# The RWKV stage's projections as three fp32r products, with both parts kept in DRAM

## The chip, the cores and the metric

One core of a Trainium2 chip. The time is device microseconds of one execution of the whole program, the median of three runs: 3976.36 us (3972.51 to 3979.13). Engines: TensorE (PE, its weight loads PEld), VectorE (DVE), ScalarE (ACT), GpSimd (POOL) and SyncE (SP), which issues all DMAs from one queue, in order.

## The reference, cut to what matters

One step of a bidirectional hybrid trunk of two layers, on 128 context tokens and 1024 latent tokens (T = 1152 columns in all), in float32, with D = 1024:

```
def trunk_layer(x, mod, p, states, rows, rope):
    h = rmsnorm(x, norm_g) * (1 + scale) + shift            # adaLN
    u = h @ w_in                                            # 1024 -> P_IN, split into four groups
    y_a = mlstm_branch(u_a)       # 4 pairs of heads each
    y_b = rglru_branch(u_b)       # LRU
    y_c = retention_branch(u_c)
    y_d = rwkv_branch(u_d)        # r, k, v, g, and a low-rank part
    x = x + gate * (concat(y_a, y_b, y_c, y_d) @ w_out)     # 4 x 512 -> 1024
```

Each branch runs a recurrence in both directions over the tokens. The result is the last `x` after a final norm, and the context's states.

## The kernel before, in words

Activations lie as [128 features, T tokens]. The token axis is cut into three chunks of `CH3` = 384 columns. A layer has three parts.

*Input projection and three mixers.* `in_proj` makes every column tile of `u` that the first three mixers need, and those of RWKV's pair 0, in the order of the table `JOBS`. The norm leaves `h` in SBUF as two fp32r parts, `hh` and `hl`; a weight tile is loaded and split into `wring_h` and `wring_l`; each product is three fp32r matmuls (hi·hi, hi·lo, lo·hi), accumulated in PSUM: 4032 of them a layer. The tiles of `u` go to DRAM. `ml_pair`, `lr_pair` and `rt_pair` (mLSTM, LRU, retention; pairs 0 to 3 each, written in this order) read them there as they come, at a higher priority than `in_proj`. Each ends with one [128, T] tile of its result, which is stored to DRAM at `yc(m, p)`. Most of a mixer's tiles have one buffer, so its pairs follow each other; retention's pools open where the LRU's close.

*RWKV stage.* `rw_all` goes through nine units (two halves of four pairs, and one for the context). Its chain of steps on TensorE and VectorE has a fixed order on TensorE (`strict`, `chain`), and between the steps `pull` takes "fills" from the generator `work`: one `fill` is one fp32 matmul of 384 columns for one k. Fills make RWKV's own projections for pairs 1 to 3 (`late_proj`, k = 8) and the output projection (`out_proj`, first for the three mixers' 12 k tiles, then for RWKV's pairs 0 to 2), in layer 0 also the remaining modulation rows (`wmod`). Each fill's activations (`y_tile`) and weights (`w_tile`) come from DRAM, through rings of `YOB` and `OWB` buffers. 648 fills a layer, modulation aside.

*Tail.* RWKV's pair 3 is projected with the split done in place (`tail`), then the norm of the next layer or the final one.

Where instructions have no fixed order, the scheduler orders each engine's queue once, when the program is built, by priority, by its estimate of when operands are ready and by when a tile's buffer is free. A pool's buffers are handed out in the order in which the code asks for them. On the chip every queue runs in that order.

Of the kernel before, what the change touches and what calls it, by code (L numbers as in the profile page):

```python
# [19 lines left out]
KT = 8  # L20
# [10 lines left out]
class B:  # L31
# [326 lines left out]
    def rw_final(self, l, X):  # L358

        c, y, W = self.c, X["y"], X["W"]  # L360
        H = [slice(o, o + 512) for o in range(0, W, 512)]
        z = self.rf.tile([128, NST], F32, tag="yq", name="yq")[:, :W]
        for h in H:
            self.act(z[:, h], y[:, h], ACT.Square)
        self.headsum(lambda ps, h: self.act(z[:, h], ps, ACT.Ln, scale=1.0 / 64, bias=c["eps"]), z, W)
        self.act(z, z, ACT.Exp, scale=-0.5)
        for h in H:
            self.tt(self.v if X["p"] == 3 else self.g, z[:, h], z[:, h], X["A"][:, h], MUL)
            self.stt(self.v, z[:, h], z[:, h], 0.5, y[:, h], MUL, MUL)
            self.tt(self.v, y[:, h], z[:, h], X["B"][:, h], ADD)  # L370
            for p, s in X["segs"]:
                a, b = max(s.start, h.start), min(s.stop, h.stop)
                if a < b:
                    o = X["src"].start - s.start
                    self.dma(self.Y[l, 3, p][:, a + o:b + o], y[:, a:b])

    def silu2(self, t, g, out=None):

# [292 lines left out]
    def tok_norm_gate(self, pool, ps, y, p, m, gname, k2, tags, pt_tag):  # L671

        c = self.c
        sq = pool.tile([128, 18, 64], F32, tag=tags[0], name="nsq")
        yv = y.rearrange("p i (h d) -> p (i h) d", d=64)
        self.act(sq, yv, ACT.Square)
        ss = pool.tile([128, 18], F32, tag="nss", name="nss")
        self.v.tensor_reduce(out=ss, in_=sq, op=ADD, axis=AXX)
        self.act(ss, ss, ACT.Ln, scale=1.0 / (64 * k2 * k2), bias=c["eps"])
        self.act(ss, ss, ACT.Exp, scale=-0.5)  # L680
        self.tt(self.g, yv, yv, ss[:, :, None].broadcast_to([128, 18, 64]), MUL)
        g = pool.tile([128, T], F32, tag=tags[1], name="ng")
        self.dma(g, self.uc(gname, p))
        sg = sq.rearrange("p a d -> p (a d)")
        self.silu2(sg, g)
        for i0, n in ((0, 4), (4, 4), (8, 1)):
            pt = ps.tile([128, 512], F32, tag=pt_tag, name="ntr")
            for i in range(n):
                self.t.transpose(pt[:, 128 * i:128 * i + 128], y[:, i0 + i], c["ident"])
            s = slice(128 * i0, 128 * (i0 + n))  # L690
            self.stt(self.v, g[:, s], pt[:, :128 * n], 0.5 / k2, sg[:, s], MUL, MUL)
        self.dma(self.yc(m, p), g)


    def load_consts(self, pool, names):
# [314 lines left out]
    def lr_pair(self, l, p):  # L1010
# [46 lines left out]
        sg = tl("tr")  # L1057
        self.silu2(sg, g)
        self.stt(self.v, hd[0], hd[0], 0.5, sg, MUL, MUL)
        self.dma(self.yc(1, p), hd[0])  # L1060


    def open_main(self):
# [24 lines left out]
            self.par[n] = t  # L1088
        self.mod = [p.tile([128, 24, 2], F32, name="mod%d" % l) for l in range(2)]

    def mod_rows(self, l, j, pool, w, n, pr, pc, mm, between=lambda k: None):


        row_ps = pr()
        for k in range(0, 8, n):
            wt = w()
            self.dma(wt, self.i["w_mod"][l, j][:, k:k + n])
            between(k // n)
            for z in range(n):
                mm(row_ps[0:2], self.sc[:, k + z], wt[:, z], start=(k + z == 0), stop=(k + z == 7))  # L1100
                if k + z < 7:
                    yield
        row = pool.tile([2, 512], F32, tag="mrow", name="mrow", bufs=1)
        self.a.copy(row, row_ps[0:2])
        col_ps = pc()[:, 0:8].rearrange("p (i c) -> p i c", c=2)
        for i in range(4):
            self.tr(col_ps[:, i], row[:, 128 * i:128 * i + 128])
        self.tt(self.v, self.mod[l][:, 4 * j:4 * j + 4], col_ps,
                self.par["bmod"][:, 24 * l + 4 * j:24 * l + 4 * j + 4, None].broadcast_to([128, 4, 2]), ADD)
        yield  # L1110

    def modulation(self, l, j, pool):

        w = lambda: pool.tile([128, 1, 512], F32, tag="ow", name="wmod")
        yield from self.mod_rows(l, j, pool, w, 1, self.pmain, self.pmain, self.fill)

    def modulation0(self, pool, ps, between):

# [13 lines left out]
    def norm_h(self, l, xs, sg, r, hh, hl, o):  # L1132
# [10 lines left out]
                self.tt(e, hl[:, m, s], x, hh[:, m, s].bitcast(F32), SUB)  # L1143
        s = slice(o, o + CH3)
        if o == 0:
            self.H[l] = self.dr0.tile([128, KT, T], F32, name="h_%d" % l)
        self.dma(self.H[l][:, :, s], xs)

    def first_norm(self, hh, hl):
        with ExitStack() as st:  # L1150
# [27 lines left out]
    def tail(self, l, ks, open_h):  # L1178
# [3 lines left out]
        with ExitStack() as st:  # L1182
# [10 lines left out]
            yr = [tp.tile([128, CH3], F32, name="t_yr%d" % j) for j in range(3)]  # L1193
# [9 lines left out]
            for o in range(0, T, CH3):  # L1203
                c = slice(o, o + CH3)
                yh, yl = yt[o // CH3 % 2]
                for j, k in enumerate(ks):
                    raw = yr[(o // CH3 * nk + j) % 3]
                    self.dma(raw, self.Y[l, 3, k][:, c])
                    self.a.copy(yh[:, j], raw)
                    self.tt(self.v, yl[:, j], raw, yh[:, j].bitcast(F32), SUB)  # L1210
# [36 lines left out]
        self.a.copy(hi, raw)  # L1247
        self.tt(self.g, lo, raw, hi.bitcast(F32), SUB)

    def in_proj(self, l, wp, sp, hh, hl):  # L1250
        n = 0
        rh = wp.tile([128, 3, KT, 128], F32R, name="wring_h")
        rl = wp.tile([128, 3, KT, 128], F32R, name="wring_l")
        pos = 0
        for t_, (kind, name, p, tiles) in enumerate(JOBS):
            if name[:3] == "rw_" and p in LATE:
                continue
            nt = len(tiles)
            if pos + nt > 3:
                pos = 0  # L1260
# [35 lines left out]
        return self.pe(self.t.matmul(*a, **k))  # L1296

    def y_tile(self, yp, src):
        t = yp.tile([128, CH3], F32, tag="y", name="yt")
        self.dma(t, src)  # L1300
        return t

    def w_tile(self, wp, src, n=4):
        t = wp.tile([128, 4, 128], F32, tag="ow", name="ow")
        self.dma(t[:, :n], src)
        return [t[:, k] for k in range(n)]

    def proj(self, ws, ys):

        ps = self.pmain()  # L1310
        for k, (w, y) in enumerate(zip(ws, ys, strict=True)):
            self.fill(ps[:, :CH3], w, y, start=(k == 0), stop=(k == len(ws) - 1))
            if k < len(ws) - 1:
                yield
        return ps[:, :CH3]

    def late_proj(self, l, pair, wp, yp, sp):

        js = [(name, tiles[0]) for kind, name, p, tiles in JOBS if name[:3] == "rw_" and p == pair]
        for name, t in js:  # L1320
            self.U[l, name, pair] = self.dr0.tile([128, T], F32, name="u_%s_%d_%d" % (name, pair, l))
        for o in range(0, T, CH3):
            c = slice(o, o + CH3)
            ys = [self.y_tile(yp, self.H[l][:, k, c]) for k in range(KT)]
            for name, t in js:
                ws = sum((self.w_tile(wp, self.i["w_in"][l, t][:, z:z + 4]) for z in (0, 4)), [])
                xi = sp.tile([128, CH3], F32, tag="x", name="xi")
                ps = yield from self.proj(ws, ys)
                self.a.copy(xi, ps)
                self.dma(self.U[l, name, pair][:, c], xi)  # L1330
                yield
        self.done.add(pair)

    def out_proj(self, l, gs, wp, yp, sp):

        X = [self.dr0.tile([128, T], F32, name="x_%d_%d_%d" % (l, gs[0][0], m)) for m in range(8)]
        for o in range(0, T, CH3):
            c = slice(o, o + CH3)
            ys = [self.y_tile(yp, self.Y[l, g, k][:, c]) for g, n in gs for k in range(n)]
            for m in range(8):  # L1340
                ws = sum((self.w_tile(wp, self.i["w_out"][l, g, m][:, 0:n], n) for g, n in gs), [])
# [17 lines left out]
    def build(self):  # L1359
# [10 lines left out]
        for l in range(2):  # L1370
            self.uc = lambda n, p: self.U[l, n, p]
            self.ut = self.uc
            def yc(m, p):
                self.Y[l, m, p] = self.dr0.tile([128, T], F32, name="y_%d_%d_%d" % (m, p, l))
                return self.Y[l, m, p]
            self.yc = yc
            with self.ph as ph:
                P = lambda n, b=1, **kw: ph.enter_context(tc.tile_pool(name=n + "_%d" % l, bufs=b, **kw, **tw))
                wp, sp = P("w"), P("st")
                self.in_proj(l, wp, sp, *self.h)  # L1380
                with tc.high_priority(offset=HP1), ExitStack() as st:
                    Q = lambda n, b=1, **kw: st.enter_context(tc.tile_pool(name=n + "_%d" % l, bufs=b, **kw, **tw))
                    self.mlrow = self.dr.tile([2, 40, T], F32, tag="mlrow", name="mlrow")
# [23 lines left out]
            with ExitStack() as ph:  # L1407
# [9 lines left out]
                def work():  # L1417
                    for p in LATE:
                        for z, j in MODS[p] if l == 0 else ():
                            yield from self.modulation(z, j, wp)  # L1420
                        yield from self.late_proj(l, p, wp, yp, sp)
                    yield from self.out_proj(l, ((0, 4), (1, 4), (2, 4)), wp, yp, sp)
                    while self.finished < 4:
                        yield
                    yield from self.out_proj(l, ((3, 3),), wp, yp, sp)
                    self.done.add("all")

                self.fills, self.done, self.credit, self.pulled, self.finished = work(), set(), 0.0, 0, 0
# [13 lines left out]


LATE, PROMPTS = (1, 2, 3), 6
OWB, SO = 6, 3
MODS = {1: ((0, 4), (0, 5)), 2: ((1, 0), (1, 1), (1, 2)), 3: ((1, 3), (1, 4), (1, 5))}
T12 = 2
LDB = dict(ld=2, ld2=2, y=1)
HP1 = 1000000
HP2 = 2000000  # L1450
RIGHT = "right"
MLB = 1
YOB = 16
RESERVE = 44
HV = (slice(0, 64), slice(64, 128))

# [154 lines left out]
```

## Time and profile before

| | us |
|---|---|
| median of three runs | 3976.36 |
| the profiled execution | 3979.25 |
| its span, first to last instruction | 3977.5 |
| TensorE busy | 3648.6 (92%) |
| VectorE busy | 2033.8 (51%) |
| ScalarE busy | 1291.7 (32%) |
| GpSimd busy | 1110.7 (28%) |
| mean DMA rate | 135 GB/s |

A busy share is a mean over stretches with different limits; matmuls are pipelined and their ends are modelled, so the time from one start to the next is a matmul's cost where they follow each other. In the list of groups one fp32 fill counts as two instructions.

### The profile page before, as it was taken

The page shows a single profiled execution, that of the slowest core. Times are in us where ns is not written, and L with a number is a line of the kernel's source. Part 1 is how long each engine was busy: PE and PEld are TensorE (multiplying, and loading weights), DVE is VectorE, ACT ScalarE, POOL GpSimd, SP SyncE. Part 2 cuts the span into 40 slices and gives each one's busy share as a digit, 9 for nine tenths or more (in the row PEclk, how much of TensorE's full clock was granted, in tenths as well). Part 3 has the DMA queues.
Part 4 walks back from the last instruction along what each step waited for, and adds up shares of the span by engine and source line. Part 5 has one row for each costly group of instructions (what it writes and reads, how often), then busy time and mean ns, then how long its engine had stood idle before and what let it go on. Part 6 is the DMA issues. An engine that isn't in the chain of part 4 may idle for free. (4 is left out here: it accounts for less than half of the span.)

```text
span 3977.5 us, 69524 instructions
## 1 busy us (share of the span) xinstructions
PE 3648.6 (92%) x28050; PEld 2831.0 (71%) x28050; DVE 2033.8 (51%) x3953; ACT 1291.7 (32%) x2102; POOL 1110.7 (28%) x1016
## 2 busy tenths in 40 slices
PE   6899999999899999998888999999997899989997
PEld 2899889999654555555468888999996555655554
DVE  4445544332364566675364545443423566766644
ACT  3234432212223334332142434422121334343313
POOL 4233234424331222212032232344243312122200
PEclk7999899989799999999989998999897999999998
DMA  5434343433356544344653443435333444434446
GB/s 214 122 106 137 121 132 120 141 111 120 127 156 187 146 141 134 109 124 123 198 189 118 104 120 124 129 121 146 106 122 119 133 151 133 141 101 126 129 128 201
DMA packets 413550, 538.02 MB, mean 135 GB/s; under 512 B 141708, under 2 KB 322700, under 8 KB 413228
## 3 DMA queue, kind: packets, MB, share of 16 engines
q1 hardware_dynamic: 413228, 533.57, 44.5%
q8 instruction: 221, 3.62, 0.4%
q14 instruction: 101, 0.83, 0.1%
HBM read 387.17 MB, written 146.25 MB: 134 GB/s over the span
## 5 line engine op out<-in xcount | busy, mean ns | idle before, releaser
L1296 PE MATMUL main<-yt,ow 128*128 128x384 f32 x2592 | 989.0, 520 | 25.1 <-DVE xi L48 17.5
L1296 PEld LDWEIGHTS main<-yt,ow 128*128 128x128 f32 x2592 | 478.0, 197 | 328.0 <-issue 49.1
L59 PE MATMUL main<-hh,wring_h 128*128 128x384 f32 x1824 | 648.1, 356 | 25.6 <-DVE st L1290 11.5
L59 PE MATMUL main<-hl,wring_h 128*128 128x384 f32 x1824 | 647.8, 355 | 21.7 <-DVE hl L44 19.6
L59 PE MATMUL main<-hh,wring_l 128*128 128x384 f32 x1824 | 644.1, 353 | 0.0
L44 POOL TENSOR_TENSOR wring_l<-raw,wring_h 128x1024 fp32r<-128x1024 f32 x100 | 246.8, 2472 | 605.1 <-ACT wring_h L1247 457.7
L59 PEld LDWEIGHTS main<-hh,wring_h 128*128 128x128 f32 x1824 | 360.8, 198 | 39.0 <-DVE st L1290 10.1
L59 PEld LDWEIGHTS main<-hl,wring_h 128*128 128x128 f32 x1824 | 361.1, 198 | 33.8 <-DVE hl L44 22.4
L59 PEld LDWEIGHTS main<-hh,wring_l 128*128 128x128 f32 x1824 | 360.7, 198 | 8.7 <-issue 2.7
L59 PE MATMUL main<-wring_h,hh 128*128 128x256 f32 x864 | 265.0, 307 | 17.7 <-DVE st L1290 17.1
L59 PE MATMUL main<-wring_h,hl 128*128 128x256 f32 x864 | 261.2, 302 | 0.0
L59 PE MATMUL main<-wring_l,hh 128*128 128x256 f32 x864 | 260.4, 301 | 0.0
L44 POOL TENSOR_TENSOR t<-s_k,bb 128x512 f32<-128x512 f32 x36 | 62.4, 1734 | 570.4 <-ACT bb L56 570.4
L1290 DVE COPY st<-main 128x384 f32<-128x384 f32 (+1 forms) x168 | 86.0, 512 | 261.8 <-PE main L59 222.5
L44 DVE TENSOR_TENSOR tm<-iU,iN 64x31 f32<-64x31 f32 (+15 forms) x558 | 202.2, 362 | 15.9
L44 DVE TENSOR_TENSOR iN<-iN,tm 64x31 f32<-64x31 f32 (+15 forms) x558 | 193.8, 347 | 15.8
L59 PEld LDWEIGHTS main<-wring_h,hh 128*128 128x128 f32 x864 | 178.0, 206 | 22.9 <-DVE st L1290 18.5
L59 PEld LDWEIGHTS main<-wring_h,hl 128*128 128x128 f32 x864 | 178.5, 207 | 4.5 <-issue 1.1
L59 PEld LDWEIGHTS main<-wring_l,hh 128*128 128x128 f32 x864 | 178.2, 206 | 2.7
L1247 ACT CAST wring_h<-raw 128x1024 fp32r<-128x1024 f32 x100 | 103.5, 1047 | 221.0 <-PE main L59 178.5
L1288 ACT COPY st<-main 128x384 f32<-128x384 f32 (+1 forms) x168 | 73.4, 437 | 270.2 <-PE main L59 264.3
L56 ACT ACT_TABLE_LOAD x123 | 157.8, 1283 | 2.9 <-PEq L1603 0.7
(332 smaller groups left out, 6040.2 us busy)
## 6 DMA issues: line engine op xcount, KB each, us to landing
raw<-in_w_in SPq DMA_DIRECT2D x100, 512.0 KB
ow<-in_w_in SPq DMA_DIRECT2D x144, 256.0 KB
ow<-in_w_out SPq DMA_DIRECT2D x144, 256.0 KB
yt<-h SPq DMA_DIRECT2D x144, 192.0 KB
mrb<-mlrow SPq DMA_DIRECT2D x48, 384.0 KB
x<-xi SPq DMA_DIRECT2D x96, 192.0 KB
yt<-y SPq DMA_DIRECT2D x90, 192.0 KB
wmod<-in_w_mod SPq DMA_DIRECT2D x64, 256.0 KB
```

The lines of the kernel that those rows point to most:

```text
L44: return e.tensor_tensor(out=out, in0=a, in1=b, op=op)
L56: return self.a.activation(out=out, in_=a, func=f, scale=scale, bias=bias)
L59: return self.t.matmul(out, l, r, start=start, stop=stop)
L1247: self.a.copy(hi, raw)
L1288: self.a.copy(q[:, :w], ps[:, :w])
L1290: self.v.tensor_copy(q[:, :w], ps[:, :w])
L1296: return self.pe(self.t.matmul(*a, **k))
```

## The change

The fp32 fill becomes three fp32r matmuls, whose parts are made once and kept in DRAM.

- `norm_h` stores `hh` and `hl` in place of `h`; the DRAM tile has a part axis.
- The three mixers store through the new `put_y`: a cast to fp32r in a tile of the new pool `yh` (one buffer), a subtraction in place, two stores. `rw_final` does the same by halves.
- `split_work` splits the 56 weight pieces a layer that the fills use; `in_proj` takes two a job.
- `y_tile` and `w_tile` load both parts; the rings become 10 and 4 buffers of twice the size.
- The output projection's groups are 8 and 7 k tiles (mLSTM and LRU, then retention and RWKV's pairs 0 to 2) in place of 12 and 3.
- `t12` and the RWKV loads `ld` go from two buffers to one; the modulation row uses a buffer of the weight ring; the tail loads the two parts.

```diff
@@ rw_final
+            hi, lo = z[:, h].bitcast(F32R), y[:, h].bitcast(F32R)
+            self.a.copy(hi, y[:, h])
+            self.tt(self.v, lo, y[:, h], z[:, h], SUB)
...
@@ tok_norm_gate, and the same in lr_pair with self.put_y(1, p, hd[0])
-        self.dma(self.yc(m, p), g)
+        self.put_y(m, p, g)
@@ norm_h
-            self.H[l] = self.dr0.tile([128, KT, T], F32, name="h_%d" % l)
-        self.dma(self.H[l][:, :, s], xs)
+            self.H[l] = self.dr0.tile([128, KT, 2, T], F32, name="h_%d" % l)
+        for j, x in enumerate((hh, hl)):
+            self.dma(self.H[l][:, :, j, s], x[:, :, s].bitcast(F32))
@@ new
+    def split_work(self, l, pool):
+        srcs = [((t, z), self.i["w_in"][l, t][:, 4 * z:4 * z + 4]) for q in LATE for kind, name, p, tiles in JOBS
+                if name[:3] == "rw_" and p == q for t in tiles for z in range(2)]
+        srcs += [((g, m, "out"), self.i["w_out"][l, g, m]) for g in range(4) for m in range(8)]
+        self.W = {}
+        for n, (key, src) in enumerate(srcs):
+            raw = pool.tile([128, 4, 128], F32, tag="sraw", name="sraw")
+            hi, lo = (pool.tile([128, 4, 128], F32R, tag="s" + x, name="s" + x) for x in ("hi", "lo"))
+            self.dma(raw, src)
+            self.a.copy(hi, raw)
+            self.tt(self.v, lo, raw, hi.bitcast(F32), SUB)
+            self.W[key] = self.dr0.tile([128, 2, 4, 128], F32, name="ws_%d_%d" % (l, n))
+            self.dma(self.W[key][:, 0], hi.bitcast(F32))
+            self.dma(self.W[key][:, 1], lo.bitcast(F32))
+            yield
+    def put_y(self, m, p, y):
+        hi = self.yhp.tile([128, T], F32R, tag="yhi", name="yhi")
+        self.a.copy(hi, y)
+        lo = y.bitcast(F32R)
+        self.tt(self.v, lo, y, hi.bitcast(F32), SUB)
+        dst = self.yc(m, p)
+        self.dma(dst[:, 0], hi.bitcast(F32))
+        self.dma(dst[:, 1], y)
@@ in_proj, once a job
+            for _ in range(2):
+                next(splits, None)
@@ y_tile, w_tile, proj
-        t = yp.tile([128, CH3], F32, tag="y", name="yt")
+        t = yp.tile([128, 2, CH3], F32, tag="y", name="yt")
...
-        t = wp.tile([128, 4, 128], F32, tag="ow", name="ow")
-        self.dma(t[:, :n], src)
+        t = wp.tile([128, 2, 4, 128], F32, tag="ow", name="ow")
+        self.dma(t[:, :, :n], self.W[key][:, :, :n])
...
-            self.fill(ps[:, :CH3], w, y, start=(k == 0), stop=(k == len(ws) - 1))
+            for j, (a, b) in enumerate(((wh, yh), (wh, yl), (wl, yh))):
+                self.pm(ps[:, :CH3], a, b, start=(k + j == 0), stop=(k == len(ws) - 1 and j == 2))
+            self.pulled += 1
@@ work
-                    yield from self.out_proj(l, ((0, 4), (1, 4), (2, 4)), wp, yp, sp)
+                    yield from self.out_proj(l, ((0, 4), (1, 4)), wp, yp, sp)
...
-                    yield from self.out_proj(l, ((3, 3),), wp, yp, sp)
+                    yield from self.out_proj(l, ((2, 4), (3, 3)), wp, yp, sp)
@@ build
-                wp, sp = P("w"), P("st")
-                self.in_proj(l, wp, sp, *self.h)
+                wp, sp, self.yhp = P("w"), P("st"), P("yh")
+                self.in_proj(l, wp, sp, P("ws"), *self.h)
@@ constants
-OWB, SO = 6, 3
+OWB, SO = 4, 3
-T12 = 2
-LDB = dict(ld=2, ld2=2, y=1)
+T12 = 1
+LDB = dict(ld=1, ld2=2, y=1)
-YOB = 16
+YOB = 10
```

What the change does to the queues shows at three places, all of layer 0. The first is SP's queue where LRU pair 0 stores its result (`y_1_0_0`: mixer 1, pair 0, layer 0). Before, with mLSTM pair 0 (`y_0_0_0`) behind it:

```order
L81 DMA y_1_0_0_6910<-lr_h_6864 128x1152
L81 DMA u_ml_k_1_0_1466<-st_1492 128x384
L81 DMA u_ml_k_1_0_1466<-st_1520 128x384
L81 DMA u_ml_k_1_0_1466<-st_1548 128x384
L81 DMA lr_xb_6995<-u_lr_g_1_0_1288 128x1152
L81 DMA mk_5793<-u_ml_k_1_0_1466 128x1152
L81 DMA ut_ml_vo_1_0_1559<-st_1585 128x256
L81 DMA raw_1990<-in_w_in 128x1024
L81 DMA ut_ml_vo_1_0_1559<-st_1613 128x256
L81 DMA ut_ml_vo_1_0_1559<-st_1641 128x256
L81 DMA y_0_0_0_5785<-ng_5766 128x1152
```

With the change, at the same store of its high part (`yhi`):

```order
L81 DMA u_rt_q_3_0_5153<-st_5235 128x384
L81 DMA raw_5594<-in_w_in 128x1024
L81 DMA u_rt_k_3_0_5242<-st_5268 128x384
L81 DMA y_0_3_0_7303<-yhi_7300 128x1152
L81 DMA y_0_3_0_7303<-ng_7281 128x1152
L81 DMA u_rt_k_3_0_5242<-st_5296 128x384
L81 DMA y_1_0_0_7442<-yhi_7439 128x1152
L81 DMA c_rw_mu_8745<-in_p_rw_mu 128x13
```

The store moved from ahead of mLSTM pair 0 (`y_0_0_0`) to behind mLSTM pair 3 (`y_0_3_0`), where the projection already stores tiles of the last retention pair (`u_rt_q_3`, `u_rt_k_3`).

The second place is TensorE's queue at the end of the input projection (`main<-hh,wring_h` and its like are projection matmuls; rkt, rup, rS and rN are retention's, lrg the LRU's). Before:

```order
L59 MATMUL main<-hl,wring_h 128x384
L59 MATMUL main<-hh,wring_l 128x384
L59 MATMUL main<-hh,wring_h 128x384
L59 MATMUL rup<-rtV,rkw 128x64 x6
L59 MATMUL main<-hl,wring_h 128x384
L59 MATMUL main<-hh,wring_l 128x384
L954 MATMUL rkt<-ident,rtk 128x128 x3
L59 MATMUL rup<-rtV,rkw 128x64 x6
L59 MATMUL rS<-rtq,rtk 128x128 x3
L59 MATMUL rN<-rtV,rsd 128x64 x3
```

With the change:

```order
L59 MATMUL main<-hh,wring_h 128x384
L59 MATMUL main<-hl,wring_h 128x384
L59 MATMUL main<-hh,wring_l 128x384
L59 MATMUL lrg<-lr_xc,lr_gw 128x384 x15
L958 MATMUL rkt<-ident,rtk 128x128
L59 MATMUL rS<-rtq,rtk 128x128
L958 MATMUL rkt<-ident,rtk 128x128 x2
L59 MATMUL rS<-rtq,rtk 128x128 x2
L59 MATMUL rup<-rtV,rkw 128x64 x6
L958 MATMUL rkt<-ident,rtk 128x128 x3
```

Before, this is the last of four retention pairs; with the change it is the first, and the other three follow it with no projection matmul between.

The third place is TensorE's queue in the RWKV stage, where unit 0's scores (`a<-AR,BK`) alternate with fills (`main<-yt,ow`). Before:

```order
L59 MATMUL a<-AR,BK 128x128 x8
L1296 MATMUL main<-yt,ow 128x384 x3
L59 MATMUL a<-AR,BK 128x128 x8
L1296 MATMUL main<-yt,ow 128x384 x3
L59 MATMUL a<-AR,BK 128x128 x8
```

With the change:

```order
L59 MATMUL a<-AR,BK 128x128 x8
L59 MATMUL main<-yt,ow 128x384 x9
L59 MATMUL a<-AR,BK 128x128 x8
L59 MATMUL main<-yt,ow 128x384 x9
L59 MATMUL a<-AR,BK 128x128 x8
```

The number of fills between two steps stays; each is three matmuls.

## Rows read from the trace of the kernel before

**Rows 1.** Windows by stage; columns: stretch, busy (instructions), PEclk, DMA share, GB/s.

```profile
56.00:1041.00 985.00, 936.40 (x5561) 879.42 (x5562) 445.33 (x675) 309.32 (x451) 364.49 (x351) 0.93 0.41 123
1041.00:1087.00 46.00, 28.62 (x124) 25.20 (x126) 8.76 (x13) 7.52 (x11) 12.54 (x23) 0.55 0.37 122
1090.00:1935.00 845.00, 780.49 (x7962) 456.67 (x7962) 508.88 (x1179) 285.45 (x526) 170.10 (x127) 0.96 0.47 139
1970.00:1990.00 20.00, 14.69 (x29) 7.60 (x30) 8.14 (x10) 6.28 (x7) 6.67 (x3) 0.73 0.95 320
3029.00:3075.00 46.00, 29.20 (x124) 25.78 (x126) 8.76 (x13) 7.45 (x11) 12.51 (x23) 0.53 0.37 122
3080.00:3934.00 854.00, 774.88 (x8094) 476.33 (x8093) 523.40 (x1215) 287.08 (x524) 167.30 (x127) 0.96 0.47 138
```

**Rows 2.** Timeline, TensorE, RWKV stage: start, duration, what, number.

```profile
1515.99 2.85 PE L1296 MATMUL main<-yt,ow 128*128 128x384 f32 x8
...
1519.05 2.20 PE L1296 MATMUL main<-yt,ow 128*128 128x384 f32 x6
```

**Rows 3.** Timeline, TensorE, two matmuls of the input projection.

```profile
700.14 0.33 PE L59 MATMUL main<-hl,wring_h 128*128 128x384 f32 x1
700.32 0.33 PE L59 MATMUL main<-hh,wring_l 128*128 128x384 f32 x1
```

**Rows 4.** Groups by line, TensorE: number | busy, mean ns | idle before, releasers.

```profile
L1296 PE MATMUL main<-yt,ow 128*128 128x384 f32 x2592 | 989.0, 520 | 25.1 <-DVE xi L48 17.5 <-ACT xi L1329 3.7 <-PE main L1296 3.2
...
L59 PE MATMUL lrg<-lr_xc,lr_gw 128*128 128x384 f32 x192 | 85.5, 528 | 6.6 <-DVE lr_xc L48 5.8 <-ACT lr_ti L56 0.8
...
L59 PE MATMUL rN<-rtV,rsd 128*128 128x64 f32 x288 | 65.8, 322 | 0.1
...
L59 PE MATMUL rN<-rtR,rtQX 128*128 128x64 f32 x256 | 60.3, 325 | 6.6 <-POOL rtR L44 6.6
...
L59 PE MATMUL rS<-rtq,rtk 64*128 64x128 f32 x288 | 55.2, 330 | 3.1 <-DVE rsd L44 3.1
```

**Rows 5.** Timeline, last retention pair of layer 0, VectorE and GpSimd.

```profile
1007.30 0.28 DVE L48 SCALAR_TENSOR_TENSOR ng<-ntr,nsq 128x128 f32<-128x128 f32 x1
...
1019.45 3.23 POOL L44 TENSOR_TENSOR rtk<-rtk,rt_xs 128x1024 f32<-128x1024 f32 x1
1022.76 6.04 POOL L44 TENSOR_TENSOR rtQX<-rtq,rtXI 64x1024 f32<-64x1024 f32 x2
...
1041.53 1.02 DVE L44 TENSOR_TENSOR rkw<-rkt,rt_wk 128x384 f32<-128x384 f32 x2 [2.99 <-PE rkt L954]
...
1086.24 0.29 DVE L48 SCALAR_TENSOR_TENSOR ng<-ntr,nsq 128x128 f32<-128x128 f32 x1 [0.57 <-PE ntr L689]
```

**Rows 6.** Timeline, LRU pair 3 of layer 0, its first and last operation.

```profile
482.55 1.35 ACT L56 ACTIVATE lr_xc<-lr_xb,c_lr_cb,c_lr_cw 128x1152 f32<-128x1152 f32 x1 [1.34 <-DMA lr_xb<-u_lr_x]
...
556.12 1.55 DVE L48 SCALAR_TENSOR_TENSOR lr_h<-lr_h,lr_tr 128x1152 f32<-128x1152 f32 x1 [2.57 <-POOL lr_h L44]
```

**Rows 7.** DMA issues of the fills, both layers: number, KB each.

```profile
ow<-in_w_in SPq DMA_DIRECT2D x144, 256.0 KB
ow<-in_w_out SPq DMA_DIRECT2D x144, 256.0 KB
yt<-h SPq DMA_DIRECT2D x144, 192.0 KB
...
yt<-y SPq DMA_DIRECT2D x90, 192.0 KB
...
ow<-in_w_out SPq DMA_DIRECT2D x48, 192.0 KB
```

**Rows 8.** Timeline, casts and elementwise operations of the shapes nearest to the added ones.

```profile
1073.01 1.16 ACT L56 ACTIVATE nsq<-rty 128x1152 f32<-128x1152 f32 x1
...
1078.55 1.36 DVE L48 SCALAR_TENSOR_TENSOR nsq<-nsq,ng 128x1152 f32<-128x1152 f32 x1 [2.92 <-ACT nsq L56]
...
1990.82 0.51 ACT L1209 CAST t_yh<-t_yr 128x384 fp32r<-128x384 f32 x1 [13.28 <-DMA t_yr<-y]
1991.37 0.56 DVE L44 TENSOR_TENSOR t_yl<-t_yr,t_yh 128x384 fp32r<-128x384 f32 x1 [2.37 <-ACT t_yh L1209]
```

More of the change, by code (lines that the diff above doesn't have):

```diff
@@ L374, in rw_final @@
                     o = X["src"].start - s.start
-                    self.dma(self.Y[l, 3, p][:, a + o:b + o], y[:, a:b])
+                    for j, x in enumerate((z, y)):
+                        self.dma(self.Y[l, 3, p][:, j, a + o:b + o], x[:, a:b])
     def silu2(self, t, g, out=None):
@@ L1059, in lr_pair @@
         self.stt(self.v, hd[0], hd[0], 0.5, sg, MUL, MUL)
-        self.dma(self.yc(1, p), hd[0])
+        self.put_y(1, p, hd[0])
     def open_main(self):
@@ L1089, in params, with mod_rows @@
         self.mod = [p.tile([128, 24, 2], F32, name="mod%d" % l) for l in range(2)]
-    def mod_rows(self, l, j, pool, w, n, pr, pc, mm, between=lambda k: None):
+    def mod_rows(self, l, j, pool, w, n, pr, pc, mm, between=lambda k: None, row=None):
         row_ps = pr()
@@ L1096, in mod_rows @@
             wt = w()
-            self.dma(wt, self.i["w_mod"][l, j][:, k:k + n])
+            self.dma(wt[:, :n], self.i["w_mod"][l, j][:, k:k + n])
             between(k // n)
@@ L1102, in mod_rows @@
                     yield
-        row = pool.tile([2, 512], F32, tag="mrow", name="mrow", bufs=1)
+        row = row()[0:2, 0] if row else pool.tile([2, 512], F32, tag="mrow", name="mrow", bufs=1)
         self.a.copy(row, row_ps[0:2])
@@ L1112, in modulation @@
     def modulation(self, l, j, pool):
-        w = lambda: pool.tile([128, 1, 512], F32, tag="ow", name="wmod")
-        yield from self.mod_rows(l, j, pool, w, 1, self.pmain, self.pmain, self.fill)
+        w = lambda: pool.tile([128, 2, 512], F32, tag="ow", name="wmod")
+        yield from self.mod_rows(l, j, pool, w, 1, self.pmain, self.pmain, self.fill, row=w)
     def modulation0(self, pool, ps, between):
@@ L1192, in tail @@
             yt = [[tp.tile([128, nk, CH3], F32R, name="t_y%s%d" % (n, j)) for n in "hl"] for j in range(2)]
-            yr = [tp.tile([128, CH3], F32, name="t_yr%d" % j) for j in range(3)]
             xs = [xp.tile([128, KT, CH3], F32, name="xs%d" % j) for j in range(3)]
@@ L1206, in tail @@
                 for j, k in enumerate(ks):
[L1207 to L1210, printed above, removed]
+                    self.dma(yh[:, j].bitcast(F32), self.Y[l, 3, k][:, 0, c])
+                    self.dma(yl[:, j].bitcast(F32), self.Y[l, 3, k][:, 1, c])
                 x = xs[o // CH3]
@@ L1248, in split_w, with in_proj @@
         self.tt(self.g, lo, raw, hi.bitcast(F32), SUB)
-    def in_proj(self, l, wp, sp, hh, hl):
+    def split_work(self, l, pool):
[21 more added lines that the diff above has]
+        self.dma(dst[:, 1], y)
+    def in_proj(self, l, wp, sp, mp, hh, hl):
         n = 0
+        splits = self.split_work(l, mp)
         rh = wp.tile([128, 3, KT, 128], F32R, name="wring_h")
@@ L1298, in y_tile, with w_tile @@
     def y_tile(self, yp, src):
-        t = yp.tile([128, CH3], F32, tag="y", name="yt")
+        t = yp.tile([128, 2, CH3], F32, tag="y", name="yt")
         self.dma(t, src)
-        return t
-    def w_tile(self, wp, src, n=4):
-        t = wp.tile([128, 4, 128], F32, tag="ow", name="ow")
-        self.dma(t[:, :n], src)
-        return [t[:, k] for k in range(n)]
+        return t[:, 0].bitcast(F32R), t[:, 1].bitcast(F32R)
+    def w_tile(self, wp, key, n=4):
+        t = wp.tile([128, 2, 4, 128], F32, tag="ow", name="ow")
+        self.dma(t[:, :, :n], self.W[key][:, :, :n])
+        return [(t[:, 0, k].bitcast(F32R), t[:, 1, k].bitcast(F32R)) for k in range(n)]
     def proj(self, ws, ys):
         ps = self.pmain()
-        for k, (w, y) in enumerate(zip(ws, ys, strict=True)):
-            self.fill(ps[:, :CH3], w, y, start=(k == 0), stop=(k == len(ws) - 1))
+        for k, ((wh, wl), (yh, yl)) in enumerate(zip(ws, ys, strict=True)):
+            for j, (a, b) in enumerate(((wh, yh), (wh, yl), (wl, yh))):
+                self.pm(ps[:, :CH3], a, b, start=(k + j == 0), stop=(k == len(ws) - 1 and j == 2))
+            self.pulled += 1
             if k < len(ws) - 1:
@@ L1323, in late_proj @@
             c = slice(o, o + CH3)
-            ys = [self.y_tile(yp, self.H[l][:, k, c]) for k in range(KT)]
+            ys = [self.y_tile(yp, self.H[l][:, k, :, c]) for k in range(KT)]
             for name, t in js:
-                ws = sum((self.w_tile(wp, self.i["w_in"][l, t][:, z:z + 4]) for z in (0, 4)), [])
+                ws = sum((self.w_tile(wp, (t, z)) for z in range(2)), [])
                 xi = sp.tile([128, CH3], F32, tag="x", name="xi")
@@ L1338, in out_proj @@
             c = slice(o, o + CH3)
-            ys = [self.y_tile(yp, self.Y[l, g, k][:, c]) for g, n in gs for k in range(n)]
+            ys = [self.y_tile(yp, self.Y[l, g, k][:, :, c]) for g, n in gs for k in range(n)]
             for m in range(8):
-                ws = sum((self.w_tile(wp, self.i["w_out"][l, g, m][:, 0:n], n) for g, n in gs), [])
+                ws = sum((self.w_tile(wp, (g, m, "out"), n) for g, n in gs), [])
                 xi = sp.tile([128, CH3], F32, tag="x", name="xi")
@@ L1373, in yc @@
             def yc(m, p):
-                self.Y[l, m, p] = self.dr0.tile([128, T], F32, name="y_%d_%d_%d" % (m, p, l))
+                self.Y[l, m, p] = self.dr0.tile([128, 2, T], F32, name="y_%d_%d_%d" % (m, p, l))
                 return self.Y[l, m, p]
```

## The prediction

> **What bounds the kernel now.** I read the windows by stage first [rows 1]. Each layer has three stretches. From 56 to 1041 us the input projection's matmuls and the three mixers that follow it (mLSTM, LRU, retention) share TensorE, which is busy 936 of 985 us; the mixers' long chains on VectorE, ScalarE and GpSimd lie beside 4032 projection matmuls and cost little. From 1041 to 1087 (layer 1: 3029 to 3075) the projection is used up, the last half retention pair runs alone, TensorE is busy 29 of 46 us and its granted clock falls from 0.93 to 0.55, towards the lower of its two levels. From 1087 on is the RWKV stage: TensorE 780 of 845 us, DMA share 0.47. So TensorE sets the pace wherever projection matmuls stand next to a chain, and a mixer's own chain sets it where none do. The change touches both.
>
> **The fills of the RWKV stage get shorter.** Now a fill (one k of a late projection or output projection) is two instructions. In the timeline a group of eight takes 2.85 us and one of six 2.20 [rows 2], so one instruction takes 0.325 us and a fill 0.65. The fp32r matmul of the same 384 columns starts every 0.173 us [rows 3], so three take 0.52. There are 2592 halves in both layers [rows 4], 648 fills a layer: 648 x 0.13 = 84 us, 88 at the granted 0.96. That is the most a layer can gain here.
>
> **The same fills fetch twice the bytes.** Per layer [rows 7]: weights 72 x 256 KB twice and 24 x 192 KB, 42.5 MB; activations 117 x 192 KB, 23.0 MB. So 65.5 MB more. The fullest stretch moves 320 GB/s at a share of 0.95, 337 at 1. The stage's DMA time goes from 0.47 x 845 = 397 to 397 + 194 = 591 us, in a stage of 845 - 88 = 757: a mean share of 0.78, and it comes in lumps. Of a chunk's 8 activation tiles only 2 find one of the 10 buffers free; the other 6 (2.36 MB, 7.0 us) and two weight tiles (1.05 MB, 3.1 us) must land in the time of about ten fills, 10 x 757/648 = 11.7 us, on an SP queue that also carries the triangular solve's transfers and is held by the first load that waits for its buffer. Before, 16 buffers held two of a late projection's chunks. There are 15 chunk starts in a layer: from none stalling (-88 us) to each losing the 7.0 (105 - 88 = +17). No row shows such a stall, so I take half the gain, -44 per layer, and keep both ends. The single buffers for u (`ld`), `t12` and the shorter weight ring I cost at 0: a block's three loads have eight gaps of the chain, some 30 us, before they are used; uncovered they are in the +17.
>
> The Trainium skill ("DMA: Bandwidth & Descriptors", Specifications) gives a core about 358 GB/s from HBM. By that the stage's 183 MB would take 510 us, a share of 0.67, and I would take -60 instead of -44, a total of 4363; the fullest row here shows 320, so the sum stays with the row.
>
> **The mixers lose their cover.** This is the large term, and it follows from the order, not from a duration. `put_y` takes its high part from a pool with one buffer. Buffers are handed out in the order of the code: mLSTM pairs 0 to 3, then LRU 0 to 3, then retention 0 to 3. LRU pair 0, which before stored its result ahead of mLSTM pair 0, now waits for the buffer until mLSTM pair 3 has stored; behind it wait LRU pair 1 (its `h` tiles are single), then LRU 2 and 3, and retention, whose pools open when the LRU's close. On SP the store of LRU pair 0 stands behind that of mLSTM pair 3, when the projection is already storing the last retention keys. On TensorE, where retention now stands among the last projection matmuls, the changed kernel has all projection matmuls, then 15 LRU matmuls and then all four retention pairs without one projection matmul among them; the RWKV stage's first matmul follows the last pair, as before. Layer 1 has the same order.
>
> Per layer, step by step. (a) The projection ends sooner, since what leaves it no longer runs there: the rN and rS matmuls take 181 us in both layers, 91 a layer, with rup's on top; some 25 of these lie in the 46 us already bare; 15 of 48 LRU matmuls are 13 more [rows 4]. These groups overlap each other's modelled ends, so I take 75 (bounds 60 and 90). (b) A bare retention pair: from the last gate of pair 2 (1007.58) to that of pair 3 (1086.53) are 79 us [rows 5]. Its three groups of transposes and updates stood among projection matmuls, from 1022.7 to the end of the last rkw at 1042.6, 20 us; most of the recursion, the two-sided sums and the gate behind them were bare already. Bare, a group is rkw's 1.0 us and some three times that for its transposes, its updates and their copy, 12 for three, so 79 - 8 = 71; the cast and subtraction that `put_y` adds to a [128, 1152] tile, 1.2 and 1.4 us by the nearest rows [rows 8], partly beside the next pair's loads, make it 72. Its buffers are single, so pairs don't overlap: 4 x 72 = 288. (c) LRU pair 3 took 75 us beside the projection [rows 6]; with nothing beside it I take 60, and 15 for the end of pair 2. Together 363 us bare, in which TensorE does little and runs near its lower level, as in the bare row, from which (b) is taken. Against it stand the 46 us bare now and the 75 of (a): 363 - 46 - 75 = +242.
>
> The bounds of the bare stretch: 4 x 60 + 60 = 300 if a pair sheds its waits; 4 x 79 + 90 = 406 if it sheds none.
>
> **What else is added** lies in the projection stretch. 56 weight pieces a layer, each a cast and a subtraction of [128, 512]: by the [128, 384] rows, 0.51 and 0.56 us [rows 8], times 4/3, 38 us on ScalarE and 42 on VectorE; `put_y` adds 12 x 1.2 and 12 x 1.4. Both engines are under half busy there (309 and 445 of 985 us), so TensorE's matmuls hide it. 168 transfers of 44 MB and the second parts of h and y raise the DMA share from 0.41 to some 0.58. I charge 10 us a layer for evictions that queue behind such an operation (0 to 25). In the tail a cast and a subtraction go and `rw_final` gets them instead: 0.
>
> **Sum.** Against the profiled execution's own 3979.25 us (span 3977.5, 1.75 around it; 0.07% over the median of the runs): 3979 + 2 x (242 + 10 - 44) = **4395 us**, 10% slower.
>
> **Rivals.**
> - *Transfers bind the RWKV stage too* (chance 0.20). Every chunk start waits, and the stage gives back its gain: +17 in place of -44, 3979 + 2 x (252 + 17) = 4517. For it: 0.78 mean share and two buffers of slack. Against: at 0.47 the fills' idle time names no transfer among its releasers [rows 4].
> - *The bare stretch is shorter* (0.17). With the engines to themselves the mixers shed their waits: 300 instead of 363, 4395 - 126 = 4269. For it: TensorE's own matmuls interleave badly with projection ones now. Against: most of the 79 us were bare already.
> - *The kernel gets faster* (0.03). Place: the same stretch. The change wins if the bare mixers take no more than 46 + 75 + 44 - 10 = 155 us a layer, 120 say: 3979 + 2 x (120 - 46 - 75 + 10 - 44) = 3909. That needs LRU and retention to run side by side, or `put_y`'s buffer to come free early enough that the order costs nothing. Against: the matmuls are in one queue in that order, and a pair's GpSimd work alone (6.0 us for rtQX, 3.2 for one of three rtk steps [rows 5], then the recursion) fills much of 155 when taken four times.
>
> **Numbers.** The forecast has 0.60. Its own spread is the bare stretch (-63 to +43 a layer), the RWKV term (-44 to +61) and the smaller ones. 4250 to 4530 holds most of the forecast, all of the second rival and most of the first. A measurement of this kernel tells about 0.2% (8 us) from no change; slower 0.96, same 0.01, faster 0.03.
>
> **What would show it.** Right: after the last projection matmul of each layer a stretch of some 360 us with a granted clock near 0.55 and TensorE busy about half, four rtQX clusters in it; the RWKV stage starting near 1340; a stage of about 800 us with fp32r starts 0.173 us apart and a DMA share above 0.7. Wrong in size: a bare pair of 60 or of 80. Wrong altogether: retention matmuls among projection matmuls, or a RWKV stage that starts before 1150.

## The result, and the profile after

The changed kernel takes **4605.81 us** (median; 4598.44 to 4611.9), the kernel before beside it 3974.88: a ratio of 1.1575, 95% interval [1.1547, 1.1602]. The forecast was 4395, its range 4250 to 4530. The direction and the large term were right; the time is 211 us over the forecast, and outside the range.

The windows of the changed kernel answer to [rows 1], in the same columns: projection, bare stretch and RWKV stage of the first layer, then the last two of the second.

```profile
58.00:980.00 922.00, 858.35 (x5020) 810.73 (x5021) 362.16 (x597) 276.30 (x403) 259.45 (x235) 0.92 0.53 162
980.00:1389.00 409.00, 185.32 (x669) 145.06 (x668) 119.62 (x157) 85.55 (x124) 113.08 (x138) 0.50 0.27 77
1389.00:2340.00 951.00, 790.46 (x8905) 614.48 (x8904) 534.43 (x1237) 302.22 (x547) 173.92 (x130) 0.90 0.68 217
3260.00:3667.00 407.00, 185.99 (x671) 145.62 (x670) 119.83 (x158) 85.89 (x124) 112.89 (x138) 0.50 0.27 81
3667.00:4559.00 892.00, 732.84 (x8744) 609.32 (x8743) 533.20 (x1225) 293.78 (x534) 171.38 (x127) 0.89 0.65 208
```

The bare stretch of 46 us is now 409 and 407, at a granted clock of 0.50, the lower level. The RWKV stage is longer than before, though TensorE is busy for less of it.

VectorE's timeline shows the four bare retention pairs, each by the start of its last gate operation; they answer to the first and last row of [rows 5].

```profile
1153.65 0.29 DVE L48 SCALAR_TENSOR_TENSOR ng<-ntr,nsq 128x128 f32<-128x128 f32 x1 [0.57 <-PE ntr L693]
...
1233.29 0.29 DVE L48 SCALAR_TENSOR_TENSOR ng<-ntr,nsq 128x128 f32<-128x128 f32 x1 [0.57 <-PE ntr L693]
...
1311.46 0.29 DVE L48 SCALAR_TENSOR_TENSOR ng<-ntr,nsq 128x128 f32<-128x128 f32 x1 [0.57 <-PE ntr L693]
...
1386.08 0.29 DVE L48 SCALAR_TENSOR_TENSOR ng<-ntr,nsq 128x128 f32<-128x128 f32 x1 [0.57 <-PE ntr L693]
```

They lie 79.6, 78.2 and 74.6 us apart, 77.5 in the mean, where the forecast had 72.

The group of the fills, for [rows 4], with the idle time before them:

```profile
L59 PE MATMUL main<-yt,ow 128*128 128x384 f32 x3888 | 870.5, 370 | 69.3 <-DMA ow<-ws 35.1 <-DMA yt<-y 15.6 <-DMA yt<-h 15.3
```

Transfers, which released next to none of the fills' idle time before (0.2 us of the matmuls' own), now release most of it. TensorE's timeline shows that the fills themselves have the pace of [rows 3]:

```profile
1644.61 1.85 PE L59 MATMUL main<-yt,ow 128*128 128x384 f32 x9
...
1647.65 2.38 PE L59 MATMUL main<-yt,ow 128*128 128x384 f32 x12
```

Three more matmuls take 0.53 us more, 0.177 each. So the fills are faster, and the stage is not.

### The profile page after: what moved, and what is told of

The parts are those of the page before. It is cut to its first block, busy times and chain, and to the rows that moved or that the text cites. A ratio compares the mean times of both kernels' runs of the same rounds, so it can differ in the third digit from the quotient of the medians.

```text
span 4603.2 us, 73366 instructions
## 1 busy us (share of the span) xinstructions
PE 3694.0 (80%) x29346; PEld 3176.1 (69%) x29346; DVE 2096.9 (46%) x4101; ACT 1392.3 (30%) x2250; POOL 1099.8 (24%) x1016
## 5 line engine op out<-in xcount | busy, mean ns | idle before, releaser
L59 PE MATMUL main<-yt,ow 128*128 128x384 f32 x3888 | 870.5, 370 | 69.3 <-DMA ow<-ws 35.1
L59 PEld LDWEIGHTS main<-yt,ow 128*128 128x128 f32 x3888 | 715.7, 203 | 132.3 <-issue 35.0
L59 PE MATMUL main<-wring_h,hh 128*128 128x256 f32 x864 | 253.5, 293 | 24.9 <-DVE st L1322 14.9
L59 PE MATMUL main<-wring_l,hh 128*128 128x256 f32 x864 | 250.5, 290 | 0.0
L59 PE MATMUL main<-wring_h,hl 128*128 128x256 f32 x864 | 250.2, 290 | 0.0
L44 DVE TENSOR_TENSOR iN<-iN,tm 64x31 f32<-64x31 f32 (+15 forms) x558 | 211.3, 379 | 14.0
L44 DVE TENSOR_TENSOR slo<-sraw,shi 128x512 fp32r<-128x512 f32 x112 | 96.7, 863 | 238.7 <-ACT shi L1262 238.6
L59 PE MATMUL lrg<-lr_xc,lr_gw 128*128 128x384 f32 x192 | 109.1, 658 | 108.9 <-DVE lr_xc L48 51.9
L958 PE MATMUL rkt<-ident,rtk 128*128 128x128 f32 x72 | 23.5, 441 | 193.8 <-DMA rtk<-u_rt_k 110.1
```

The source lines that it names most:

```text
L44: return e.tensor_tensor(out=out, in0=a, in1=b, op=op)
L59: return self.t.matmul(out, l, r, start=start, stop=stop)
L958: self.t.transpose(pt[:, i], k[:, 128 * (g + i):128 * (g + i) + 128], c["ident"])
```

## The experiments

Two questions: whether the one buffer of `put_y` alone makes the bare stretch, and what eats the gain of the fills. All times of one stage below are from the profiled execution of each kernel, in us, first layer and second: the projection from its first to its last matmul; bare, from there to the last retention gate, or to the end of `put_y`'s subtraction where one follows it; RWKV, from there to the first matmul of the tail; then the tail's matmuls, in the first layer those ahead of the next projection (in the changed kernel 54 of 72; the other 18 stand in the projection).

| kernel | median | projection | bare | RWKV | tail |
|---|---|---|---|---|---|
| before | 3975 | 984, 996 | 46, 46 | 905, 859 | 40, 26 |
| changed | 4606 | 922, 900 | 409, 406 | 951, 892 | 18, 25 |
| e1_own_hi | 4134 | 1046, 1018 | 50, 52 | 949, 897 | 19, 25 |
| e2_before_one_buffer | 4493 | 897, 894 | 392, 396 | 902, 869 | 40, 26 |
| e3_half_bytes | 4040 | 1032, 1025 | 50, 50 | 894, 862 | 17, 27 |
| e4_one_product | 4110 | 1029, 1030 | 50, 52 | 935, 883 | 20, 28 |
| e5_solve_queue | 4176 | 1035, 1022 | 52, 50 | 964, 925 | 19, 25 |
| e6_old_buffers | 4024 | 1031, 1019 | 51, 53 | 876, 858 | 35, 25 |
| e7_fp32_fills | 4137 | 1037, 1031 | 51, 53 | 968, 879 | 20, 26 |
| e9_no_splits | 4063 | 1011, 998 | 51, 50 | 936, 887 | 18, 25 |
| e10_short_solve | 3928 | 1026, 1026 | 52, 52 | 838, 796 | 35, 25 |
| e11_before_short_solve | 3954 | 974, 995 | 46, 47 | 894, 842 | 41, 26 |
| e12_high_only | 3974 | 1012, 1009 | 46, 46 | 858, 858 | 30, 27 |

### The one buffer

**e1_own_hi** takes the buffer away.

```diff
-        hi = self.yhp.tile([128, T], F32R, tag="yhi", name="yhi")
+        hi = spare.bitcast(F32R)        # put_y(m, p, g, sg), put_y(1, p, hd[0], sg)
```

> The changed kernel with put_y's high part in a tile the mixer already owns and no longer needs (the gate's sg), so that no pool of one buffer ties mLSTM, LRU and retention together. Theory (the one buffer moves LRU and retention behind the projection; 402 to 406 us bare a layer): retention stands among projection matmuls again, a bare stretch of 40 to 70 us, the RWKV stage starts at 1085 to 1120, and with the gain of the RWKV stage given back the whole is 3979 + 2 x (10 + 15) = about 4030 (3990 to 4090). Rival (put_y's work and the doubled transfers themselves make the mixers long): over 4400.

4134.47, a ratio of 1.0389 [1.0359, 1.0419]: 471 us come back. The windows show the bare stretch gone:

```profile
58.00:1105.00 1047.00, 955.68 (x5550) 890.78 (x5551) 496.99 (x738) 348.79 (x512) 376.95 (x350) 0.91 0.55 167
1105.00:1155.00 50.00, 32.64 (x140) 27.56 (x139) 10.10 (x15) 10.19 (x15) 12.54 (x23) 0.56 0.36 121
```

The total is 104 over what was expected and outside its range. The projection stretch grew by 62 and 22 us, not by 10 each, which is 64 of it; stage and tail grew by 23 and 37, not by 15 each, which is 30.

**e2_before_one_buffer** adds the buffer and ScalarE's copy into it (1.1 us a pair), and nothing else, to the kernel before. The edit is in the results of all three mixers, though the expectation names two.

```diff
-        self.dma(self.yc(m, p), g)
+        hi = self.yhp.tile([128, T], F32, tag="yhi", name="yhi")   # the pool's one buffer
+        self.a.copy(hi, g)
+        self.dma(self.yc(m, p), hi)
```

> The kernel before, with one thing added: LRU's and retention's results are copied by ScalarE into a one-buffer pool and stored from there; no splits, no second parts, the old RWKV stage. Theory: the bare stretch comes back alone, 390 to 400 us a layer against 46, projection ending 60 earlier: 3976 + 2 x (395 - 46 - 60) = about 4555 (4480 to 4620), with the RWKV stage as before, 905. If put_y's subtraction and second store make a bare pair 78 us rather than 72, the pairs here take 72 and the total is some 50 less. Rival (the buffer alone is harmless): 3980 to 4000.

4492.66, a ratio of 1.1288 [1.1255, 1.1322]: 517 us from one buffer and its copy, with the RWKV stage as it was. Its windows over the projection and the bare stretch:

```profile
57.00:954.00 897.00, 849.78 (x5021) 805.84 (x5022) 315.88 (x537) 251.26 (x353) 255.60 (x235) 0.94 0.36 110
954.00:1346.00 392.00, 180.42 (x664) 143.06 (x663) 117.32 (x150) 80.24 (x119) 117.94 (x138) 0.51 0.25 72
```

The projection ends 87 and 102 us sooner, 94 in the mean, more than the 75 that were taken. The gates of its four pairs start 75.9, 76.6 and 73.3 us apart, 75.3 in the mean. So a bare pair is 75 without `put_y`'s subtraction and second store. The two more of the changed kernel are put down to these, by one trace of each; the subtraction alone is 1.4.

### The fills' gain

**e3_half_bytes** halves what e1 loads in the RWKV stage.

```diff
-        self.dma(t, src)
-        return t[:, 0].bitcast(F32R), t[:, 1].bitcast(F32R)
+        self.dma(t[:, 0], src[:, 0])
+        return t[:, 0].bitcast(F32R), t[:, 0].bitcast(F32R)      # w_tile likewise
```

> e1_own_hi with only the high part of weights and activations loaded in the RWKV stage and used in all three products; the lower parts' share of the result is left out. As many matmuls, buffers and loads as in e1_own_hi, half the bytes. Theory (the doubled bytes give back the fills' gain, by late solve and weight transfers): the stage shrinks by 60 to 85 us a layer, the total is 120 to 170 below e1_own_hi, DMA share of the stage near 0.4, and the waits for the solve's return (SC<-dN) go. Rival (fewer buffers, or fp32r products that start slower among other matmuls): within 30 of e1_own_hi.

4039.79: 95 us under e1, less than expected; the stage shrinks by 55 and 35. The waits for the solve's return (`SC<-dN`, the transfers that bring the triangular solve's result back to TensorE's operand) do not go (23 and 51 us, against 43 and 48 in e1). The bytes are part of it, not all.

**e5_solve_queue** moves the solve's transfers to ScalarE.

```diff
-        self.dma(dN[f], N[f])
+        self.a.dma_start(dN[f], N[f])        # and the other 19 transfers of rw_solve
```

> e1_own_hi with the triangular solve's 22 transfers a block issued by ScalarE instead of SyncE. If they are late because they stand behind fill loads in SyncE's queue: TensorE's waits for SC<-dN (30 and 40 us) go and the total falls by 40 to 80. If the transfers are slow because the DMA engines are full, or because ScalarE now waits at the issues and evicts late: within 20 of e1_own_hi, or slower.

The edit moves 20 transfers a block, not 22. 4175.58, 41 us slower than e1, and the waits for SC<-dN are 46 and 59 us against 43 and 48. Another queue does not remove the waits. Whether ScalarE's own waits at the issues add the 41 us was not separated.

**e4_one_product** takes most of TensorE's work out of the fills.

```diff
-            for j, (a, b) in enumerate(((wh, yh), (wh, yl), (wl, yh))):
-                self.pm(ps[:, :CH3], a, b, start=(k + j == 0), stop=(k == len(ws) - 1 and j == 2))
+            self.pm(ps[:, :CH3], wh, yh, start=(k == 0), stop=(k == len(ws) - 1))
```

> e1_own_hi with one fp32r product a fill in place of three; the lower parts' share of the result is left out. Same bytes, buffers and loads, 1296 matmuls a layer fewer: 1296 x 0.173 = 224 us of TensorE less. If TensorE's own work still sets the RWKV stage (949 us in the first layer, 897 in the second): it shrinks by some 200 a layer. If transfers and the recurrence's own chain set it (theory): by less than 80, and idle time grows from 162 us to over 250.

4109.53 in a single run. The stage loses 14 us a layer of the 224:

```profile
1138.00:2073.00 935.00, 636.56 (x7609) 428.22 (x7609) 545.39 (x1239) 302.41 (x548) 182.17 (x130) 0.76 0.68 221
3177.00:4060.00 883.00, 583.12 (x7449) 425.43 (x7447) 541.82 (x1226) 293.46 (x535) 179.67 (x127) 0.72 0.65 209
```

TensorE is busy 637 and 583 us, against 784 and 735 in e1, and the time stays. The freed time became idle time (298 and 300 us against 165 and 162 in e1), at a lower granted clock.

**e7_fp32_fills** goes the other way: e1 with the old fill.

```diff
+            self.fill(ps[:, :CH3], wh, yh, start=(k == 0), stop=(k == len(ws) - 1))   # as f32, in place of the three
```

> e1_own_hi with the old fill, one fp32 product of the high parts (two instructions, 0.65 us), on the new bytes and buffers; the lower parts' share is left out. If TensorE's work sets the stage, it grows by 84 to 88 a layer and the total by 170. If transfers and the chain set it: the extra 0.13 us a fill lies in what is idle now, and the total is within 60 of e1_own_hi (4134).

4137.37, 3 us over e1. The stage is 19 longer in one layer and 18 shorter in the other. In this RWKV stage three fp32r products are worth nothing over the one fp32 product.

**e6_old_buffers** is e3 with every buffer and group as before, so that its RWKV stage differs from the old one in its fills and in `rw_final`'s casts, subtractions and second stores (ScalarE is busy 6 and 5 us more, VectorE 3 and 11).

```diff
-OWB, SO = 4, 3
+OWB, SO = 6, 3
-T12 = 1
-LDB = dict(ld=1, ld2=2, y=1)
+T12 = 2
+LDB = dict(ld=2, ld2=2, y=1)
-YOB = 10
+YOB = 16            # tiles of one part; groups of 12 and 3
```

> e3_half_bytes with the buffers and groups of the kernel before: 16 activation tiles, 6 weight tiles, two buffers for u and t12, groups of 12 and 3; the lower parts' share is left out. So the RWKV stage differs from the kernel before in nothing but fills of three fp32r products. If bytes and fewer buffers eat the whole gain: the stage is 88 shorter than before's 905 and 859, the total 60 to 100 below e3_half_bytes (4040). If the shorter fills themselves leave the solve's latency uncovered (rival): 870 to 895 and 840 to 860, the total within 40 of e3_half_bytes.

4023.53, 16 under e3. Stage and tail together are 911 and 883 against 945 and 885 before: shorter fills, with neither bytes nor fewer buffers against them, gain 34 and 2 us, not 88 each. The rival named there holds. The second layer's stage shows where the gain went, first in the kernel before, then in e6:

```profile
3074.00:3933.00 859.00, 779.88 (x8099) 478.43 (x8099) 525.42 (x1218) 289.69 (x529) 167.98 (x127) 0.95 0.47 137
3122.00:3980.00 858.00, 708.72 (x8745) 592.45 (x8746) 535.91 (x1226) 294.25 (x536) 175.55 (x127) 0.92 0.47 141
```

TensorE is busy 71 us less in a stage of the same length; in the first layer it is busy 67 us less (828 to 761) and idle 39 us more. Of the 109 us of added idle time in both layers, 78 are waits for the solve's return.

**e10_short_solve** and **e11_before_short_solve** shorten the suspected bound, in e6 and in the kernel before.

```diff
-        for j in range(31, 0, -1):
+        for j in range(31, 15, -1):
```

> e6_old_buffers (old bytes and buffers, fp32r fills) with the triangular solve cut from 31 steps to 16, so that about half of its 31 to 48 us of VectorE work is left out in each of nine blocks a layer, some 16 x 9 = 145 us; its result is not the inverse. If the recurrence's chain sets the RWKV stage there: 60 to 130 us shorter a layer (from 876 and 858), total 3760 to 3900. If TensorE or the transfers set it: within 30 of 4023.

> The kernel before, with the same solve cut to 16 steps. If its stage (905 and 859) is set by TensorE: within 20 a layer of before. If by the chain as much as by TensorE: 30 to 70 shorter a layer. The gain of shorter fills should come out where the chain is no longer in the way: e11 less e10 in the RWKV stage near the 84 to 88 a layer that TensorE's work differs by, where it is 29 and 1 with the whole solve. Rival (fp32r fills gain nothing for another reason): the difference stays under 30.

3928.33 (ratio 0.9884 [0.9860, 0.9909]) and 3953.53 (0.9940 [0.9911, 0.9969]). e10's total is over what was expected: half of the steps are only some 90 us of VectorE's busy time (534 to 444 in the mean of the two stages; 527 to 443 from before to e11). They are worth 38 and 62 us with the short fills, and 11 and 17 with the old ones. The stages of e11 and e10 differ by 56 and 46 us, where before and e6 differ by 29 and 1. That lies between the 84 to 88 and the 30 that e11's expectation named. Its 11 and 17 are within the 20 that the same expectation gave for a stage set by TensorE: in the kernel before, the chain stood close behind TensorE and not in front of it. With half the steps TensorE's busy time falls by 70 and 66 us from e11 to e10, much as with the whole solve, but 51 of it in the mean come through, against 15. So the solve was in the way of most of the fills' gain; what holds the rest back stays open (the scheduler also orders each kernel's queues anew, which no run separates).

TensorE's waits for the last transfer of the solve, whole kernels (total us, times, longest), first the kernel before, then the changed one, e6 and e12; in e10 and e11 there is no such row, and in e4 they come to 215.8:

```profile
PE v L59 <- DMA SC<-dN: 8.0, 5, 3.4
```

```profile
PE v L59 <- DMA SC<-dN: 70.6, 29, 13.1
```

```profile
PE v L59 <- DMA SC<-dN: 86.5, 30, 15.4
```

```profile
PE v L59 <- DMA SC<-dN: 287.8, 46, 27.6
```

The less TensorE has to do beside the solve, the longer it waits for it, at half the bytes (e6, e12) too. The row names a transfer, but since a shorter solve takes the row away (e10) and half the bytes do not (e3), what is late is the whole solve, of which this transfer is the last link.

How close the solve was can be read from the kernel before. In the timeline of one block, the solve's last copy and its first user:

```profile
1516.33 1.04 ACT L522 COPY iU<-iN 32x1024 f32<-32x1024 f32 x1
...
1534.67 0.75 PE L59 MATMUL v<-ident,SC 32*32 32x32 f32 x64
```

The same two in e6:

```profile
1559.72 1.04 ACT L526 COPY iU<-iN 32x1024 f32<-32x1024 f32 x1
...
1567.32 0.25 PE L59 MATMUL v<-ident,SC 32*32 32x32 f32 x4
...
1569.19 0.91 PE L59 MATMUL v<-ident,SC 32*32 32x32 f32 x60 [1.62 <-DMA SC<-dN]
```

Before, TensorE came for the result 17 us after the copy's end; in e6 it came after 7 and had to wait. Over the 18 blocks the median of this distance is 15.3 us before, 9.6 in the changed kernel, 5.4 in e6 and 2.7 in e12. Where TensorE stood waiting, about 2.6 is the distance, which is what the return to its first operand takes.

The median hides what matters. A block's fills lose 648 x 0.13 / 9 = 9.4 us, so that a block whose distance before was over 12 has room for it. Seven of the 18 had less, two in the first layer (6.7, 9.3) and five in the second (8.3, 11.3, 3.6, 5.9, 7.8), and at these seven stand 78 of the 86 us that e6 waits. This fits a gain of 34 us in the first layer and of 2 in the second.

### The splits, and a smallest version

**e9_no_splits** leaves 55 of the 56 splits out of e1.

```diff
+            if n:
+                self.W[key] = self.W[srcs[0][0]]
+                continue
```

> e1_own_hi with one weight piece a layer split and stored instead of 56, and every fill loading that piece; the other weights' share is left out. The RWKV stage has the same work. If the 56 casts, subtractions and 168 transfers hold up the projection's evictions: the projection stretch (1046 and 1018 us against 984 and 996 before) falls by 30 to 50 a layer, the total by 60 to 100. Rival (the second parts of h and y, or the mixers' casts): within 25 of e1_own_hi.

4062.92, 72 us under e1; the projection stretch is 35 and 20 shorter, so the splits cost it that much when all three mixers stand beside it. That they do so by holding up evictions is shown in part: in the first layer the projection's waits for evictions by VectorE and ScalarE are 14.9 and 3.5 us before, 34.8 and 12.5 in e1, and 28.7 and 3.6 without the splits, which is 15 of the 35.

**e12_high_only** keeps high parts alone, on e6.

```diff
-            self.dma(self.W[key][:, 1], lo.bitcast(F32))     # and the second parts of h and y
...
+            self.pm(ps[:, :CH3], wh, yh, start=(k == 0), stop=(k == len(ws) - 1))
```

> e6_old_buffers with only high parts stored, loaded and multiplied: one cast for each weight piece and each mixer result, no subtraction, no second part of h, one fp32r product a fill (the precision of the RWKV stage's projections is that of fp32r). It has the fewest bytes and the least work of all. If the chain sets the RWKV stage, one product gives only 10 to 20 a layer over e6; with half the split work gone from the projection stretch (20 to 40 in both layers) the total is 3940 to 4000, no clear gain on 3976. If TensorE set it: under 3700.

3974.21, a ratio of 0.9990 [0.9971, 1.0010], the same as before, at lower precision. Stage and tail are 888 and 885 against 945 and 885. No kernel tried here that does the whole solve beats the kernel before.

## Why the prediction was right and wrong

- **The order and its cost: right.** One buffer handed out in program order moves LRU and retention behind the projection. e2 shows it alone (517 us), e1 takes it back (471).
- **The bare stretch: 363 forecast, 408 measured**, just over the upper bound of 406. Of the 45 us, some 22 are four pairs of 77.5 rather than 72. The estimate of 4 us for a bare group of transposes and updates was low: the three rkw operations of the pair after the first gate start at 1171.50, 1176.97 and 1182.44, 5.5 apart. Most of the other 23 lie ahead of the first pair. From the last projection matmul (980) to the first pair's last gate (1153.65) are 174 us, which less a pair of 77.5 leaves 96, where step (c) took 60 for LRU pair 3 and 15 for the end of pair 2, together 75. By their last subtractions on VectorE, pair 2 ends at 1003.8 and pair 3 at 1063.4: 23 and 60 us. The other 13 are retention's own start, for which nothing had been charged.
- **The projection ending sooner: 75 forecast, 94 in e2.** The matmuls that left took more of that stretch with them than their busy time between projection matmuls suggested.
- **What else is added: 10 forecast, 25 and 6 measured**, as the changed kernel's projection less e2's (922 - 897, 900 - 894). Near enough there; in e1, where LRU and retention stand beside it, the same work costs 62 and 22.
- **The RWKV stage: -44 forecast, +24 and +32 measured** with the tail (969 and 917 against 945 and 885). This step failed, and it is the largest: 72 of the 103 us a layer that the sum missed (45 - 19 + 5 + 72). The step is "That is the most a layer can gain here", 88, taken in full as the gain before the transfers' cost: it holds if TensorE alone sets the stage however short the fills get. But the recurrence's solve stood close behind TensorE, in seven of 18 blocks with less room than the 9.4 us that a block's fills lose, and e6 gets 18 of the 88 in the mean. The other half of the term came out near: half the gain, 44, was taken off for late transfers and smaller rings, and e1's stage and tail are 57 and 39 us over e6's, 48 in the mean, 45 of them by the bytes (e1 less e3). That was luck, as the 44 was chosen as the middle between two ends. Together 48 - 18 = +30, which is what e1 shows, and the changed kernel +28. The rival "Transfers bind the RWKV stage too" gave +17, near the time but with half of the cause.
- **The pace of a fill: right.** In the changed kernel's first RWKV stage the fills' matmuls start 0.174 us apart in the median, where the sum took 0.173. What failed is what a shorter fill is worth.
- **The rate of the transfers** was not the limit as a mean: the stage moves 217 and 208 GB/s, under the 320 of the fullest row in [rows 1]. Half of the bytes still gave back 45 us a layer (e3), and the fills of the changed kernel wait 66 us for their loads, so single loads came late. By the figure that the Trainium skill gives ("DMA: Bandwidth & Descriptors", Specifications), the forecast would have taken -60 for the RWKV term, further from what was measured.

The range was too narrow because the RWKV term was bounded from TensorE's side alone: its end of +17 still counted the full 88 as gained.

## What to carry to other kernels

A temporary with one buffer in a path shared by independent chains is an order: list who asks for it in program order before asking what it costs. A busy share of 0.92 does not say what a faster engine gains, even where that engine sets the pace: look for the slack of the longest side chain, from its last operation to the first user of its result, block by block and not in the median, and let no faster filler gain more in a block than that. And a wait named after a transfer can mean a late chain that ends in one: halve the bytes, and see whether the wait goes.

## What was not expected of the hardware

- The granted clock fell where TensorE had less to do and the time did not change: 0.91 and 0.88 in e1's two RWKV stages, 0.76 and 0.72 in e4's, of the same length within 2%.
- GpSimd's step of rtk took one of two times, and what went with it was VectorE's work beside it, not the bare stretch. It took 3.23 us before [rows 5] and 2.34 in three of the four bare pairs of a layer, but 3.20 in the first of the four and in all eight bare pairs of e2. Of the 24 such steps in the traces of before, e2 and the changed kernel, the 14 of 3.20 to 3.27 had VectorE's own part of rtQX, a product of [64, 1024] elements, running beside them for 1.0 us or more, and the ten of 2.34 to 2.40 had not.
